# The first two modulation chunks as plain float32 products with the weights stationary

## The chip, the core and the metric

The kernel runs on one core of a Trainium2 chip. Its engines are TensorE (PE, matrix products, with PEld for its weight loads), VectorE (DVE), ScalarE (ACT), GpSimd (POOL) and SyncE (SP, which here issues transfers). The metric is the device time of one execution in microseconds (us).

## The reference, cut to what matters

One layer of a hybrid backbone: a modulation vector is computed from the conditioning vector, the latent tokens (512 x 1024) and the context tokens (256 x 1024) are normalized and modulated with it, and everything else (attention, a gating MLP, gates, a retrieval of experts) works on the result.

```python
sh1, sc1, g1, sh2, sc2, g2 = jnp.split(
    (jax.nn.silu(c) @ ada_w[layer] + ada_b[layer])[:, None, :], ADA_CHUNKS, axis=-1)
csh1, csc1, cg1, csh2, csc2, cg2 = jnp.split(
    jax.nn.silu(c_ctx) @ ada_w[layer] + ada_b[layer], ADA_CHUNKS, axis=-1)
w = w_in[layer]
h = modulate(rmsnorm(x, norm1_g[layer]), sh1, sc1)
hc = modulate(rmsnorm(ctx, norm1_g[layer]), csh1, csc1)
q, k, v, gu, gv, ga, gb = jnp.split(h @ w, IN_SPLITS, axis=-1)
```

The change concerns the first two of the six parts of the modulation, sh1 and sc1 (each 1024 wide), for two vectors at once: silu(c) and silu(c_ctx). It is a product of 2 x 1024 with 1024 x 2048.

## The kernel before

The kernel computes float32 products in three reduced ones: each operand is split into hi (rounded to the format fp32r, in which PE takes one pass) and lo (the rest), and the helper `mm3` (lines 86 to 88) adds hi\*hi, hi\*lo and lo\*hi in PSUM. `split` (lines 82 and 83) makes the two: ACT rounds, DVE subtracts.

The first stage goes by eight chunks c of 128 channels. `load_ada` fetches for each chunk two tiles `raw` of 512 KB (128 x 4 x 256: four blocks of 128 input channels, and in each the 128 columns of sh1 and the 128 of sc1 of this chunk); 8 such buffers exist. `ada_first(c)` makes the chunk's modulation: it splits both tiles, and PE multiplies them as the moving operand (256 columns) with `s4` as the stationary one, in which columns 0 and 1 hold hi of the two vectors, 2 and 3 their lo, and the other 124 zeros. The result is a row tile with 4 used partitions; ACT copies it to SBUF (line 170), and two products with `fold` (line 173) turn it into columns and add the lo part. DVE adds the bias into `mod1` (line 174) and makes the scale `a1` (line 176).

Before that stage, x is loaded, normalized (`norm`, lines 237 and 239) and transposed by PE (line 302); ACT and DVE copy the transposes into `xT` in turn (lines 304 and 306). `mod_x` then makes hh and hl, the hi and lo of the modulated chunk (lines 264 to 266). For each chunk PE makes 12 products of 512 columns (`o_gu`, weights `wh`, `wl`) and 12 of 256 columns (half of `o_gv`, weights `vh`, `vl`). `ada_first(c + 2)` is a generator whose steps stand between the products of chunk c. Behind the stage stand the transposes of the context (line 250), the other half of `o_gv`, and the projections of v, k and q. `gate` is a copy of the last modulation on POOL, behind which POOL issues the loads of the other four parts of the modulation (`araw`); DVE multiplies those by itself (lines 202 and 204).

The order on each engine is not that of the code: the framework places each instruction by a timeline of its own, and each engine then runs its list in that order. SP issues the loads in its list's order, and a load waits there for its buffer.

Of the kernel before, what the change touches and what calls it, by code (L numbers as in the profile page):

```python
# [9 lines left out]
F32 = mybir.dt.float32  # L10
F32R = mybir.dt.float32r
# [4 lines left out]
AF = mybir.ActivationFunctionType  # L16
OP = mybir.AluOpType
# [4 lines left out]
P = 128  # L22
# [3 lines left out]
NC8 = D // P  # L26
# [17 lines left out]
def f(ap):  # L44
    return ap.bitcast(F32)


def body(tc, A, out):
    nc = tc.nc
    pe, dve, act, pool, sp = nc.tensor, nc.vector, nc.scalar, nc.gpsimd, nc.sync  # L50
    es = ExitStack()

    def pool_(stack, name, side="left", bufs=1):
        return stack.enter_context(tc.tile_pool(name=name, bufs=bufs, side=side, reuse_waits="tile"))
# [6 lines left out]
    def ps(tag, shape=(P, 512)):  # L61

        t = psp.tile([P, 512], F32, name="ps" + tag, bufs=4 if tag == "m" else 2)
        n = int(np.prod(shape[1:]))
        v = t[:shape[0], :n]
        if len(shape) == 3:
            v = v.rearrange("p (a b) -> p a b", b=shape[2])
        return v

    ident = const.tile([P, P], F32, name="ident")  # L70
# [10 lines left out]
    def split(raw, hi, lo, sub=dve):  # L81
        act.activation(hi, raw, AF.Copy)  # L82
        return sub.tensor_tensor(lo, raw, f(hi), op=OP.subtract)  # L83
# [21 lines left out]
    def t2(dt=F32):  # L105
        return tmp.tile([P, 512], dt, name="t2", bufs=8)
# [26 lines left out]
    def load_rows(src, t):  # L133
        x = t4()
        sp.dma_start(x, src[t * P:(t + 1) * P, :])
        return x
# [3 lines left out]
    sc = const.tile([P, NC8, 2], F32, name="sc")  # L140
# [7 lines left out]
    mod1 = const.tile([P, 16, 2], F32, name="mod1")  # L148
    a1 = const.tile([P, NC8, 2], F32, name="a1")

    def load_ada(c, i):
        raw = aw.tile([P, 4, 256], F32, name="raw", bufs=8)
        sp.dma_start(raw, A["ada01"][c, i])
        return raw

    def ada_first(c):

        bank = ps("x")
        row = bank[:, :256]
        for i in range(2):  # L160
            raw = raws[c].pop(0) if c in raws else load_ada(c, i)
            hi = aw.tile([P, 4, 256], F32R, name="hi", bufs=2)
            lo = aw.tile([P, 4, 256], F32R, name="lo", bufs=2)
            split(raw, hi, lo)
            for k in range(4):
                for w in (hi, lo):
                    pe.matmul(row, s4[:, 4 * i + k, :], w[:, k, :], start=(i + k == 0 and w is hi), stop=(i * k == 3 and w is lo))
            yield
        rs = t2()
        act.activation(rs[:, :256], row, AF.Copy)  # L170
        cps = bank[:, 256:260].rearrange("p (n x) -> p n x", n=2)
        for n in range(2):
            pe.matmul(cps[:, n, :], rs[:, n * P:(n + 1) * P], fold, start=True, stop=True)
        dve.tensor_tensor(mod1.rearrange("p (n c) x -> p n c x", n=2)[:, :, c, :], cps,
                          abc[:, 0:2, c:c + 1].to_broadcast([P, 2, 2]), op=OP.add)
        dve.tensor_scalar(a1[:, c, :], mod1[:, 8 + c, :], 1.0, ng[:, 0, c:c + 1], op0=OP.add, op1=OP.mult)
        yield
# [102 lines left out]
    cl = cx.tile([P, NC8, CTX], F32R, name="cl")  # L280
    eaw = ExitStack()
    aw = pool_(eaw, "aw", "right")

    s4 = aw.tile([P, NC8, P], F32R, name="s4")
    dve.memset(f(s4), 0.0)
    act.activation(s4[:, :, 0:2], sc, AF.Copy)
    dve.tensor_tensor(s4[:, :, 2:4], sc, f(s4[:, :, 0:2]), op=OP.subtract)
    fold = aw.tile([P, 2], F32, name="fold")
    dve.tensor_tensor(fold, ident[:, 0:2], ident[:, 2:4], op=OP.add)
    xs = [load_rows(A["x"], t) for t in range(2)]  # L290
    raws = {0: [load_ada(0, i) for i in range(2)]}
    xs += [load_rows(A["x"], t) for t in range(2, NT)]
# [14 lines left out]
    for _ in ada_first(0):  # L307
        pass
# [20 lines left out]
    for _ in ada_first(1):  # L329
        pass  # L330
    mod_x(xT, *lat_h, (1,))
    for c in range(NC8):
        if c % 2 == 0:
            wh, wl = wload(A["w_in"][3, c // 2])
        if c % 4 == 0:
            vh, vl = half_weights(4, 0, c // 4)
        if c == 3:
            cxs = [load_rows(A["ctx"], t) for t in range(CTX // P)]
            for x in cxs:
                norm(x, x)  # L340
        parts = ada_first(c + 2) if c < 6 else iter(())
        for t in range(NT):
            next(parts, None)
            ts = slice(t * P, (t + 1) * P)
            mm3(o_gu[t], hh[:, c, ts], hl[:, c, ts], wh[:, c % 2], wl[:, c % 2], c == 0, c == 7)
            gv_products(o_gv, c, vh, vl, t)
        if c < 6:
            mod_x(xT, *lat_h, (c + 2,))
# [7 lines left out]
    def proj_T(src, g, ins, n=4, sub=None, tags="mmmm"):  # L356

        o = [[ps(t, (P, w)) for t in tags] for _, _, w in ins[:1]]
        for _, _, w in ins[1:]:
            o.append([x[:, i, :] for x in [ps("x", (P, 2, w)) for _ in range(2)] for i in range(2)])  # L360
        last = 2 * n - 1
        for c, wh, wl in weights(src, g, n, sub=sub):
            for i, (rh, rl, _) in enumerate(ins):
                for b in range(4):
                    bs = slice(b * P, (b + 1) * P)
                    if i == 0:
                        mm3(o[i][b], wh[:, bs], wl[:, bs], rh[:, c, :], rl[:, c, :], c == 0, c == last)
                    else:
                        mm3(o[i][b], wh[:, bs], wl[:, bs], rh[:, c, :], rl[:, c, :], c == 0 and b % 2 == 0, c == last and b % 2 == 1, True)
        return o  # L370

    def proj_N(src, g, ins):

        o = [ps("m" if i < 4 else "x") for i in range(len(ins))]
        for c, wh, wl in weights(src, g):
            for i, (lh, ll, t) in enumerate(ins):
                ts = slice(t * P, (t + 1) * P)
                mm3(o[i], lh[:, c, ts], ll[:, c, ts], wh, wl, c == 0, c == 7)
        return o
# [56 lines left out]
    o = proj_N(A["w_in"], 2, lat_N + [(ch, cl, 0), (ch, cl, 1)])  # L436
# [24 lines left out]
    for i in range(0, 8, 2):  # L461
        o = ps("xu"[i // 2 % 2], (P, 2, 256))
# [6 lines left out]
    o, = proj_T(A["w_in"], 0, lat_T, tags="mmuu")  # L469
    ql = [t4().bitcast(F32R).rearrange("p (b m r c) -> p b m r c", b=2, m=NT, r=8) for _ in range(2)]  # L470
    for b in range(4):
        for i in range(2):
            src = o[b][HALF[i]].rearrange("p (r m c) -> p m r c", r=8, m=NT)
            hi = q2[i][HALF[i], b]
# [131 lines left out]
    for n in range(2):  # L606
        o, = proj_T(A["w_in"], 7 + n, lat_T, tags=("mmmm", "uuxx")[n])
# [9 lines left out]
    for n in range(2):  # L617
        for nm, src in (("a", A["w_pa"]), ("b", A["w_pb"])):
            o, = proj_T(src, n, [(*y2[nm], S)], n=2, tags={"a": "mmmm", "b": "uuxx"}[nm])
# [40 lines left out]
    o = proj_N(A["w_out"], 0, [(m_h, m_l, t) for t in range(NT)])  # L660
# [6 lines left out]
    for p in range(2):  # L667
        o = [ps("m"), ps("m")]
# [12 lines left out]
    for p in range(2):  # L681
        if p == 0:
            o = [x[:, i] for x in [ps("x", (P, 2, 256)) for _ in range(2)] for i in range(2)]
        else:
            o = [ps("m", (P, 256)) for _ in range(4)]
# [65 lines left out]
    for g in range(4):  # L751
        if g > 0:
            o, = proj_T(A["wq"], g, [(h2h, h2l, S)], sub=pool)
# [6 lines left out]
        for t in range(NT):  # L760
            o = ps("x" if g < 3 else "m", (P, 4, P))
# [24 lines left out]
    rs = pool_(ro, "rs", "right", bufs=2)  # L786
# [129 lines left out]
    for t in range(DT):  # L916
# [4 lines left out]
        for g in range(P // TG):  # L921
            stg = rs.tile([P, P, TG], F32, name="stg")
            for u in range(TG // TB):
# [15 lines left out]
                for v in range(2):  # L939
                    o = ps("m", (P, 4, P))  # L940
# [232 lines left out]
```

## Time and profile before

| | before |
|---|---|
| median of 3 runs | 1718.19 us (1715.9 to 1718.95) |
| the profiled execution's own time | 1715.57 us |
| its span | 1713.8 us |
| busy, share of the span | PE 97%, PEld 86%, DVE 78%, ACT 41%, POOL 29% |
| mean granted clock of PE | 0.988 of 2.4 GHz |

The span goes from the first to the last instruction. PE's busy time counts the modelled ends of pipelined products, so neighbouring products overlap in it; what a product costs in a dense stretch is the distance to the start of the next one. In a row of the timeline, "x4" means that four instructions follow each other, and the brackets say how long the engine was idle before and what ended that.

### The profile page before, as it was taken

Reading aid. Unit: us, or ns where it says so; the run is one execution under the profiler, and the core shown is the slowest. Engines: PE = TensorE matmul, PEld = TensorE weight load, DVE = VectorE, ACT = ScalarE, POOL = GpSimd, SP = SyncE. Lnnn points to the kernel's source line nnn. Section 1 sums busy time; section 2 is a strip of 40 time slices with the busy share of each in tenths; the row PEclk is TensorE's granted clock in tenths of the full one; section 3 lists DMA queues with packets and bytes.
Section 4 is the critical chain, followed back from the end, with each engine's and each line's share of the span. In section 5 each row is a group of like instructions: output and inputs, shape, how many; then the busy total and the mean of one; then the engine's idle time right before and its main releaser. Section 6 shows DMA issues by size and latency. Waiting matters only on the chain.

```text
span 1713.8 us, 24752 instructions
## 1 busy us (share of the span) xinstructions
PE 1658.1 (97%) x9033; PEld 1466.4 (86%) x9033; DVE 1329.3 (78%) x2619; ACT 705.9 (41%) x1106; POOL 494.6 (29%) x362
## 2 busy tenths in 40 slices
PE   7999999999999999999599999999999999999997
PEld 6888777888888989999588888888999999999886
DVE  8687666456779999999378788788777777777885
ACT  6532555532532456565233333333333333333333
POOL 0011100000332530000244444455454454444321
PEclk9999999999999999999799999999999999999999
DMA  9377522233511435676989999999998998997892
GB/s 355 131 247 247 160 81 74 98 112 109 197 62 39 139 120 209 223 264 229 343 309 353 341 339 344 318 338 338 338 325 291 323 340 286 330 328 272 287 315 85
DMA packets 160818, 413.11 MB, mean 241 GB/s; under 512 B 13432, under 2 KB 71288, under 8 KB 157496
## 3 DMA queue, kind: packets, MB, share of 16 engines
q1 hardware_dynamic: 116112, 253.17, 42.7%
q0 software_dynamic: 42480, 154.43, 25.8%
q10 hardware_dynamic: 2104, 3.93, 0.7%
q8 instruction: 70, 1.15, 0.3%
q14 instruction: 52, 0.43, 0.1%
HBM read 375.70 MB, written 35.78 MB: 240 GB/s over the span
## 4 chain that ended last, share of the span: by engine, by line
PE 76%; DVE 13%; DMA 5%; issue 4%; ACT 1%; SPq 0%; POOL 0%; DVEq 0%; POOLq 0%; ACTq 0%
PE psu L86 10%; PE psu L88 10%; PE psu L87 10%; PE psm L86 10%; PE psm L88 10%; PE psm L87 9%; PE psx L88 4%; PE psx L87 4%; PE psx L86 4%; PE psm L943 2%; DMA araw<-in_ada 2%; DMA wgt<-gad 1%; DVE z L712 1%; DVE i L714 1%; DVE i L711 1%
## 5 line engine op out<-in xcount | busy, mean ns | idle before, releaser
L88 PE MATMUL psu<-h2h,ulo 128*128 128x384 f32 x992 | 338.2, 342 | 3.5 <-DVE ulo L83 3.4
L86 PE MATMUL psu<-h2h,uhi 128*128 128x384 f32 x992 | 338.4, 341 | 2.7 <-ACT gact L859 2.6
L87 PE MATMUL psu<-h2l,uhi 128*128 128x384 f32 x992 | 336.9, 340 | 0.0
L1009 POOL DMA_INDIRECT gx<-in_peer_u,ex x128 | 190.3, 1487 | 244.3 <-DVE gj L1019 232.4
L82 ACT ACTIVATE uhi<-uraw 128x1024 fp32r<-128x1024 f32 x126 | 133.6, 1061 | 285.1 <-PE psu L87 245.3
L1009 POOL DMA_INDIRECT gx<-in_peer_v,ex x128 | 185.4, 1448 | 189.0 <-DVE acc L1024 139.1
L87 PE MATMUL psm<-vlo,wgh 128*128 128x512 f32 x504 | 199.3, 396 | 0.1
L88 PE MATMUL psm<-vhi,wgl 128*128 128x512 f32 x504 | 197.6, 394 | 1.1 <-DVE wgl L1000 1.1
L86 PE MATMUL psm<-vhi,wgh 128*128 128x512 f32 x504 | 175.0, 393 | 19.4 <-ACT wgh L999 18.4
L86 PEld LDWEIGHTS psu<-h2h,uhi 128*128 128x128 f32 x992 | 186.9, 188 | 6.8 <-ACT gact L859 3.3
L88 PEld LDWEIGHTS psu<-h2h,ulo 128*128 128x128 f32 x992 | 186.8, 188 | 4.6 <-DVE ulo L83 3.8
L87 PEld LDWEIGHTS psu<-h2l,uhi 128*128 128x128 f32 x992 | 186.9, 188 | 3.9
L999 ACT ACTIVATE wgh<-wgt 128x384 fp32r<-128x384 f32 x126 | 65.5, 524 | 296.3 <-issue 164.3
L83 DVE TENSOR_TENSOR vlo<-vraw,vhi 128x1024 fp32r<-128x1024 f32 x126 | 154.7, 1228 | 24.9 <-ACT vhi L82 24.6
L1000 DVE TENSOR_TENSOR wgl<-wgt,wgh 128x384 fp32r<-128x384 f32 x126 | 70.2, 557 | 130.5 <-ACT wgh L999 130.4
L1024 DVE SCALAR_TENSOR_TENSOR acc<-gx,wg,acc 128x1024 f32<-128x1024 f32 x128 | 163.8, 1280 | 0.0
L82 ACT ACTIVATE vhi<-vraw 128x1024 fp32r<-128x1024 f32 x126 | 132.0, 1047 | 65.9 <-DMA vraw<-in_peer_v 36.2
L1019 DVE SCALAR_TENSOR_TENSOR gj<-gx,h2n 128x1024 bf16<-128x1024 f32 x128 | 156.0, 1218 | 0.1
L83 DVE TENSOR_TENSOR ulo<-uraw,uhi 128x1024 fp32r<-128x1024 f32 x112 | 136.8, 1221 | 15.6 <-ACT uhi L82 12.3
L86 PEld LDWEIGHTS psm<-vhi,wgh 128*128 128x128 f32 x504 | 95.5, 190 | 38.0 <-ACT wgh L999 19.1
L82 ACT ACTIVATE whi<-wraw 128x1024 fp32r<-128x1024 f32 x60 | 63.6, 1062 | 121.0 <-PE psx L87 44.3
L88 PEld LDWEIGHTS psm<-vhi,wgl 128*128 128x128 f32 x504 | 95.0, 189 | 21.3 <-DVE wgl L1000 1.4
(383 smaller groups left out, 3360.2 us busy)
## 6 DMA issues: line engine op xcount, KB each, us to landing
vraw<-in_peer_v SPq DMA_DIRECT2D x126, 512.0 KB, 6.8
uraw<-in_ut SPq DMA_DIRECT2D x124, 512.0 KB, 5.6
wd<-stg SPq DMA_DIRECT2D x24, 1024.0 KB
wr<-wd SPq DMA_DIRECT2D x45, 512.0 KB, 10.1
araw<-in_ada POOLq DMA_DIRECT2D x32, 512.0 KB, 4.9
wraw<-in_w_in SPq DMA_DIRECT2D x24, 512.0 KB, 4.5
raw<-in_ada SPq DMA_DIRECT2D x16, 512.0 KB, 10.2
wraw<-in_wq SPq DMA_DIRECT2D x16, 512.0 KB, 3.4
```

The costliest lines, as they stand in the source:

```text
L82: act.activation(hi, raw, AF.Copy)
L83: return sub.tensor_tensor(lo, raw, f(hi), op=OP.subtract)
L86: pe.matmul(o, lh, rh, start=first, stop=False, skip_group_check=shared)
L87: pe.matmul(o, lh, rl, start=False, stop=False, skip_group_check=shared)
L88: return pe.matmul(o, ll, rh, start=False, stop=last, skip_group_check=shared).ins
L711: dve.max_index(idx[:, 0:8], val[:, 0:8], src)
L943: pe.matmul(o[:, x, :], eb_[:, 2 * v + x // 2, :, x % 2], oa[n][:, 2 * v + x // 2, :, x % 2], start=(n == 0), stop=(n == 1))
L999: act.activation(wh, w, AF.Copy)
L1000: last = dve.tensor_tensor(wl, w, f(wh), op=OP.subtract)
L1009: pool.indirect_dma_start(out=t, out_offset=None, in_=src, in_offset=bass.IndirectOffsetOnAxis(ap=ex[:, k:k + 1], axis=0))
L1019: dve.scalar_tensor_tensor(junk, u, 1.0, h2n, op0=OP.mult, op1=OP.mult, accum_out=actg[:, i:i + 1])
L1024: dve.scalar_tensor_tensor(acc, v, wg[:, i:i + 1], acc, op0=OP.mult, op1=OP.add)
```

## The change

`ada_first` no longer splits the raw tiles. The raw float32 weights become the stationary operand, 128 x 128 at a time, and the two vectors `sc` (128 x 2 for each block) the moving one, as plain float32 products: 16 for each chunk, 8 for the half of sh1 and 8 for that of sc1. The result has the form of columns already, so the row's copy and the fold go, and with them `s4` and `fold`. The first tile is held until the second is there.

```diff
     def ada_first(c):
 
-        bank = ps("x")
-        row = bank[:, :256]
+        o = ps("x", (P, 2, 2))
         for i in range(2):
             raw = raws[c].pop(0) if c in raws else load_ada(c, i)
-            hi = aw.tile([P, 4, 256], F32R, name="hi", bufs=2)
-            lo = aw.tile([P, 4, 256], F32R, name="lo", bufs=2)
-            split(raw, hi, lo)
-            for k in range(4):
-                for w in (hi, lo):
-                    pe.matmul(row, s4[:, 4 * i + k, :], w[:, k, :], start=(i + k == 0 and w is hi), stop=(i * k == 3 and w is lo))
-            yield
-        rs = t2()
-        act.activation(rs[:, :256], row, AF.Copy)
-        cps = bank[:, 256:260].rearrange("p (n x) -> p n x", n=2)
+            if i == 0:
+                held_ = raw
+                yield
         for n in range(2):
-            pe.matmul(cps[:, n, :], rs[:, n * P:(n + 1) * P], fold, start=True, stop=True)
-        dve.tensor_tensor(mod1.rearrange("p (n c) x -> p n c x", n=2)[:, :, c, :], cps,
+            for i, raw_ in enumerate((held_, raw)):
+                for k in range(4):
+                    pe.matmul(o[:, n, :], raw_[:, k, n * P:(n + 1) * P], sc[:, 4 * i + k, :], start=(i + k == 0), stop=(i * k == 3))
+            if n == 0:
+                yield
+        dve.tensor_tensor(mod1.rearrange("p (n c) x -> p n c x", n=2)[:, :, c, :], o,
                           abc[:, 0:2, c:c + 1].to_broadcast([P, 2, 2]), op=OP.add)
...
-    s4 = aw.tile([P, NC8, P], F32R, name="s4")
-    dve.memset(f(s4), 0.0)
-    act.activation(s4[:, :, 0:2], sc, AF.Copy)
-    dve.tensor_tensor(s4[:, :, 2:4], sc, f(s4[:, :, 0:2]), op=OP.subtract)
-    fold = aw.tile([P, 2], F32, name="fold")
-    dve.tensor_tensor(fold, ident[:, 0:2], ident[:, 2:4], op=OP.add)
```

The framework's order changes with it on PE, DVE, ACT and SP in the first stage; behind it each engine's list is the same but for a few moves. Line numbers of the new kernel are smaller by 4 to 11.

First place: PE from the first instruction to the products of x's transposes. t_121, t_123, t_129 and t_131 are the four normalized tiles of x. Before:

```order
L302 MATMUL psm<-ident,t_121 128x128 x4
L167 MATMUL psx<-hi,s_115 128x256
L302 MATMUL psm<-ident,t_123 128x128 x4
L167 MATMUL psx<-lo,s_115 128x256
L167 MATMUL psx<-hi,s_115 128x256
```

And with the change, where the tiles of x are called t_115, t_117, t_123 and t_125:

```order
L167 MATMUL psx<-sc,raw 128x2 x4
L291 MATMUL psm<-ident,t_115 128x128 x4
L167 MATMUL psx<-sc,raw 128x2 x7
L291 MATMUL psm<-ident,t_117 128x128 x4
L167 MATMUL psx<-sc,raw 128x2 x9
L291 MATMUL psm<-ident,t_123 128x128 x4
L291 MATMUL psm<-ident,t_125 128x128 x4
L167 MATMUL psx<-sc,raw 128x2 x10
```

The products of the modulation now stand ahead of the transposes; the 10 in the last row are chunk 1's, of which two more stand behind the other 16 transposes.

Second place: DVE from the last normalization to the first residual of hh. Before (line 83 is a split's residual, 306 a copy of transposes, 265 and 266 make hl of chunk 0):

```order
L83 TENSOR_TENSOR lo<-raw,hi 128x1024
L239 TENSOR_SCALAR t_131<-t_131,rstd_159 128x1024
L83 TENSOR_TENSOR wlo<-wraw,whi 128x1024
L306 COPY xT<-psm 128x512 x2
L83 TENSOR_TENSOR wlo<-wraw,whi 128x1024
L265 TENSOR_SCALAR t_252<-xT,a_96,mod_95 128x512
L306 COPY xT<-psm 128x512
L83 TENSOR_TENSOR lo<-raw,hi 128x1024
L306 COPY xT<-psm 128x512
L266 TENSOR_TENSOR hl<-t_252,hh 128x512
```

And with the change (the copy is line 295, hl 261 and 262, the bias 170, the scale 172):

```order
L235 TENSOR_SCALAR t_125<-t_125,rstd_153 128x1024
L170 TENSOR_TENSOR mod_95<-psx,abc 128x2x2
L172 TENSOR_SCALAR a_96<-mod_95,ng 128x2
L83 TENSOR_TENSOR wlo<-wraw,whi 128x1024
L295 COPY xT<-psm 128x512
L83 TENSOR_TENSOR wlo<-wraw,whi 128x1024
L295 COPY xT<-psm 128x512
L261 TENSOR_SCALAR t_234<-xT,a_96,mod_95 128x512
L262 TENSOR_TENSOR hl<-t_234,hh 128x512
```

The residuals of the raw tiles are gone; the two residuals of the w_in weights stay, and a copy of xT stands behind each of them.

Third place: PE among the products of chunk 2, with the change:

```order
L167 MATMUL psx<-sc,raw 128x2 x8
L86 MATMUL psm<-whi,hh 128x512
L87 MATMUL psm<-wlo,hh 128x512
L88 MATMUL psm<-whi,hl 128x512
L86 MATMUL psu<-whi,hh 128x256
L87 MATMUL psu<-wlo,hh 128x256
L88 MATMUL psu<-whi,hl 128x256
L167 MATMUL psx<-sc,raw 128x2 x8
L86 MATMUL psm<-whi,hh 128x512
```

A chunk's 16 plain products stand in two bursts of 8 with the six w_in products of one token tile between them; before, 16 products of 256 columns and a fold stood there.

## Rows read from the trace of the kernel before

**Rows 1.** Page, part 4: the chain that ended last, shares of the span.

```profile
PE 76%; DVE 13%; DMA 5%; issue 4%; ACT 1%; SPq 0%; POOL 0%; DVEq 0%; POOLq 0%; ACTq 0%
```

**Rows 2.** Groups by line and form, 0 to 80 us (busy us, mean ns).

```profile
L173 PE MATMUL psx<-fold,t 128*128 128x2 f32 x32 | 4.1, 234 | 0.5 <-ACT t L170 0.5
...
L83 DVE TENSOR_TENSOR lo<-raw,hi 128x1024 fp32r<-128x1024 f32 x16 | 19.4, 1222 | 1.5 <-DMA raw<-in_ada 0.9 <-ACT hi L82 0.5
...
L306 DVE COPY xT<-psm 128x512 f32<-128x512 f32 x4 | 2.7, 689 | 0.0
```

**Rows 3.** Timeline of PE, a stretch without waits: start us, us, engine, line, operation.

```profile
34.07 0.28 PE L167 MATMUL psx<-hi,s 128*128 128x256 f32 x1
...
35.70 0.40 PE L86 MATMUL psm<-whi,hh 128*128 128x512 f32 x1
...
36.17 0.28 PE L86 MATMUL psu<-whi,hh 128*128 128x256 f32 x1
36.29 0.28 PE L87 MATMUL psu<-wlo,hh 128*128 128x256 f32 x1
```

**Rows 4.** Timeline of ACT, then PE: the start of the w_in products.

```profile
16.93 1.06 ACT L82 ACTIVATE whi<-wraw 128x1024 fp32r<-128x1024 f32 x1 [0.45 <-DMA wraw<-in_w_in]
...
19.21 1.97 PE L302 MATMUL psm<-ident,t 128*128 128x128 f32 x16 [0.47 <-ACT xT L304]
...
21.36 0.39 PE L86 MATMUL psu<-whi,hh 128*128 128x256 f32 x1
```

**Rows 5.** Timeline of DVE, then PE: waits, and the stage's end.

```profile
28.66 0.70 DVE L266 TENSOR_TENSOR hl<-t,hh 128x512 fp32r<-128x512 f32 x1
...
51.74 0.49 PE L87 MATMUL psu<-wlo,hh 128*128 128x256 f32 x2
53.10 0.50 PE L88 MATMUL psm<-whi,hl 128*128 128x512 f32 x1 [0.87 <-DVE hl L266]
...
57.88 0.51 PE L86 MATMUL psm<-whi,hh 128*128 128x512 f32 x1 [0.37 <-ACT hh L264]
...
73.00 0.60 PE L250 MATMUL psx<-ident,t 128*128 128x128 f32 x4
```

**Rows 6.** Timeline of PE, products with one and two columns.

```profile
21.93 0.51 PE L173 MATMUL psx<-fold,t 128*128 128x2 f32 x4
22.30 0.47 PE L86 MATMUL psm<-whi,hh 128*128 128x512 f32 x1
22.61 0.39 PE L87 MATMUL psm<-wlo,hh 128*128 128x512 f32 x1
...
106.64 0.95 PE L220 MATMUL psu<-ones,t 128*128 128x1 f32 x8
107.44 0.49 PE L87 MATMUL psm<-wlo,hh 128*128 128x512 f32 x1
107.77 0.40 PE L88 MATMUL psm<-whi,hl 128*128 128x512 f32 x1
```

**Rows 7.** Page, part 6 (KB, us to landing), then timeline of DVE.

```profile
raw<-in_ada SPq DMA_DIRECT2D x16, 512.0 KB, 10.2
...
66.57 0.16 DVE L174 TENSOR_TENSOR mod<-psx,abc 128x4 f32<-128x4 f32 x1 [0.94 <-PE psx L173]
```

**Rows 8.** Timeline of DVE, then PE, 148 to 175 us.

```profile
153.02 1.37 DVE L450 SCALAR_TENSOR_TENSOR k<-psm,k 64x512 fp32r<-64x512 f32 x2 [2.92 <-ACT k L449]
...
170.97 1.54 DVE L204 SCALAR_TENSOR_TENSOR t<-araw,sc,t 128x512 f32<-128x512 f32 x2 [1.78 <-DMA araw<-in_ada]
...
174.25 0.94 PE L466 MATMUL psx<-t,t 128*128 128x128 f32 x6 [2.61 <-DVE gu L467]
```

**Rows 9.** Windows: stretch, length, busy us of each engine, PEclk, DMA share, GB/s.

```profile
176.00:178.00 2.00, 2.00 (x7) 1.52 (x6) 0.00 (x0) 0.56 (x1) 0.00 (x0) 0.50 0.18 72
```

**Rows 10.** Timeline of PE, its first products.

```profile
11.00 0.42 PE L167 MATMUL psx<-lo,s 128*128 128x256 f32 x1
11.21 0.41 PE L167 MATMUL psx<-hi,s 128*128 128x256 f32 x1
```

## The prediction

> **What bounds the kernel now.** I read the chain of waits first [rows 1]: 76% of the span ends in work of TensorE (PE), so a microsecond added to or taken from PE's line of work counts until something shows that it doesn't. The change touches the first 85 us only, so I read the groups of the first 80 us next, then PE's timeline there. In the groups [rows 2] the reader should see that one chunk's modulation costs DVE two residuals of 1.222 us (16 in all, 19.4 us), and PE 16 products of 256 columns (hi and lo) and one fold. The groups' means are no prices for PE, since its instructions overlap; its price is the distance between starts. Two products of 512 columns start 0.47 apart, so 0.235 each; 14 products of the rows 34.07 to 35.70 take 1.63, so 0.1165 each; a 256-column product of the branch weights costs 0.12, taken as 0.1175 [rows 3].
>
> Is PE the bound of the stretch that the change rewrites? From the first product with w_in (21.36) [rows 4] to the four transposes behind chunk 7 (73.00) [rows 5] is 51.64 us. In it lie 96 products of 512 columns (22.6), 96 of 256 (11.3), 95 hi and lo products (11.1), 7 folds (3.1, priced below) and 6 transposes at 0.11 (0.65): 48.7. So PE waited 2.9 us in all; the two largest waits are about 1.0 before 53.10, for hl of chunk 4 behind DVE's queue, and 0.6 before 57.88, for hh [rows 5]. DVE and ACT are late now and then, but PE is 94% of this stretch.
>
> **The change part by part.** *The split, row and fold go.* DVE loses 16 residuals and the clearing of s, ACT 16 roundings and 8 copies of the row. From 21.36 on that work lies beside PE's and is worth only PE's waits, 2.9 us. In the new order DVE reaches every hl before PE does: hl of chunk 1, behind the third weight residual in both orders, began at 28.66 with seven residuals of the modulation ahead of it [rows 5] and now comes sooner, while PE is through with chunk 0 at about 29.2 (21.4, 4.2 of w_in products, 16 plain products at 3.6); I take the full 2.9 (lower end 2.0, if the wait for the second gate-weight tile, whose buffer is freed only by chunk 3, stays in part).
>
> *PE's products.* For the six chunks after the first two, 95 hi and lo products (11.1) and 7 folds (3.1) become 96 plain products. The trace shows such a product: the fold has 16 instructions and 32 records, so two passes each, with a weight load per pass [rows 2]. A fold's four passes start at 21.93, the next product at 22.30, and the one after that 0.31 later, not 0.235: 0.445 in all, 0.111 a pass. Eight passes with one column, 106.64 to 107.77 less a 512-column product's 0.235, are 0.895, 0.112 a pass [rows 6]. The difference of the two, 0.45 for four more passes, is 0.1125, and I take that: a pass costs as much as a whole 256-column product, because a new set of weights goes in for each. The new stationary tile is 128 x 128, as there. 96 x 2 x 0.1125 = 21.6 us. Bounds: 0.0925, if the delay behind a burst (0.08) is paid once and not per pass (17.8 us); 0.1165, the hi and lo spacing (22.4 us); a load that overlapped nothing would cost more, but in no row of the bursts does it.
>
> *The start.* The order of DVE shows what decides: before PE's first w_in product come both weight residuals and two copies of xT. The second weight tile lands at 16.93, and ACT's rounding takes 1.06 [rows 4]. DVE has then done the first residual and the copy of chunk 0 (0.69 [rows 2]) by about 18.2; the second residual ends at 19.35, the copy of chunk 2 at 20.0. Only then are PE's banks free for the transposes of chunks 6 and 7 (8 x 0.109, from the 16 of the row at 19.21: 1.97 less the last one's tail [rows 4]), to 20.9, and behind them stand two products of chunk 1 (0.45): 21.35. It was 21.36. So the faster norm of the last x tile, now without residuals ahead of it, is lost behind the weights' landing; its worth is taken as 0 (between +0.5 and -1.0). The products of chunks 0 and 1 themselves cost nothing here, since they run while PE waits for x and the weights.
>
> *The raw tiles* are held until PE has used both halves. The ninth load waits for chunk 0's products (about 14), the eleventh for chunk 1's (21.4). A tile takes 10.2 us from issue to landing [rows 7], and the two are needed inside chunks 2 and 3, at about 38 and 46: hidden, with 14 us to spare. gate, which starts the other modulation's loads, hangs on chunk 7's modulation, at 66.57 so far [rows 7]; the last burst now ends inside chunk 5, at about 65. Nothing follows from that, as long as those loads don't set the end (a rival).
>
> *Sum.* 22.6 + 11.3 + 21.6 = 55.5 after, against 51.64 - 0.65 = 51.0 before (the 6 transposes move behind in the new order, at equal cost): PE leaves this stage 4.5 us later. By the bounds 0.7 to 5.3, and 6.2 with 0.9 of waits left.
>
> *Behind it.* PE is dense from 73 to 171. DVE idles 2.92 us before 153.02 until PE's key projection lets ACT go on, and from there the line runs over DVE's key copies and the next loads of the modulation to DVE at 170.97 and PE's wait of 2.61 before 174.25 [rows 8]. All of that starts from PE, so it moves with PE. Every engine's order behind the first stage is the same but for a few moves, and I found nothing tied to the clock on the wall. So +4.5 reaches the end: 1715.57 + 4.5 = 1720.1 against the profiled execution. That one was 0.15% under the median of the runs, 1718.19; on the median's scale the forecast is 1722.7 us. The three runs differ by 3 us, so about 0.2% (3.4 us) is what a measurement of this kernel can tell from no change.
>
> **The rivals.** *The shift is swallowed at 174.25 (0.19).* The chain of waits runs between 96 and 172 over the modulation's loads, not over PE. If these loads set the moment 174.25, PE's 4.5 first fills its wait of 2.61, and then the slow stretch behind it (granted clock 0.50 at 176 to 178 [rows 9]), worth some 1.7, falls away too: +0.2, so 1718.4. Against it speaks DVE's wait for PE at 153.02; for it, that the last wait of DVE (1.78 before 170.97) is for a load.
>
> *The clock (0.12).* PE's first products start 0.215 apart [rows 10], twice the later distance: PE begins at 1.2 GHz and rises at about 11.6, after 3 us of transposes and 256-column products. After the idle 2.61 us it fell again [rows 8, 9]. The new start has two-column passes and few transposes, and each chunk has two bursts of 16 such passes with 1 us of wide products between them; no row shows a burst above 8. If they don't keep the clock up, 32 products and 32 transposes of the start cost 0.215 a pass, 13.8 + 6.9 = 20.7 us from about 7.6, so chunk 0 begins 6.9 late; and two or three falls later at some 1.7 each add 4: 4.5 + 6.9 + 4 = +15, 1733. A single fall in the stage gives 1724.5. For the bursts the rows speak against it: the clock stayed up over the fold and the 8 passes.
> The Trainium skill, "TensorE: Matmul & The Clock Gate", section on HAM oscillation, tells the clock as following how busy the array has been and names idle gaps as what drops it; the rows at 174 agree, and no run here shows whether narrow passes count as busy.
>
> *Faster (0.07).* A pass is cheaper in long bursts, because its load is drawn ahead of the pass before. The point that decides is where the new passes cost what goes: 11.1 + 3.1 + 2.9 = 17.1 us over 192 passes, 0.089. At 0.06 the sum is -5.6: 1712.6. For it: a two-column pass moves next to nothing. Against it: 4 and 8 passes cost 0.111 and 0.112, with no fall.
> The skill's same page, section "Back-to-back issue gap", gives some 60 cycles for up to 64 columns, which as an estimate would be 192 x 0.025 = 4.8 us and a gain of 12; its section on LDWEIGHTS gives 128 / 1.2 = 107 ns for a load, with which the trace's 0.112 agrees.
>
> **How the numbers follow.** The forecast has 0.62. Between its bounds and with the runs' spread about a quarter of it lies under 0.2%. Slower: 0.62 x 0.77 + 0.12 = 0.60; same: 0.19 + 0.14 = 0.33; faster 0.07. The range leaves out the faster case and the clock's full price (0.19 together): from 1717.5, the swallowed shift less 1, to 1728, the upper bound of the sum (6.2) with one or two falls of the clock. The forecast's own range is 1719 to 1725.
>
> **What would show it.** Right: 256 records of two columns, spaced about 0.1125 in their bursts, 1.8 us a burst; the first w_in product at 21 to 22; no PE wait above 0.3 from there to chunk 7; chunk 7's last product about 4.5 later; PE's wait near 174 shifted to about 179 with its length unchanged. Wrong: spacing under 0.09 (faster); a wait near 174 that shrinks (swallowed); 0.215 between passes or 0.425 between 512-column products behind the first 12 us (the clock); a first w_in product well before 20, which would mean that DVE's residuals, not the weights' landing, held the start.

## The result and the profile after

The changed kernel takes 1745.21 us (median of 4 runs, 1739.47 to 1746.06), the kernel before 1718.57 beside it: ratio 1.0144, 95% interval 1.0128 to 1.0159, so 26.6 us slower. The profiled execution took 1746.06 us, 30.5 more than that of before (1715.57). The forecast was 1722.7 us: it named the direction, and lay 22.5 us too low.

The new kernel's chain that ended last, shares of the span, answers to [rows 1]: PE's share rose by two hundredths.

```profile
PE 78%; DVE 10%; DMA 5%; issue 5%; ACT 1%; POOL 0%; SPq 0%; POOLq 0%; DVEq 0%; ACTq 0%
```

The new kernel's plain products among the groups by line and form, 0 to 80 us; they stand for the three groups of [rows 2]. 256 records are 128 products of two passes.

```profile
L167 PE MATMUL psx<-sc,raw 128*128 128x2 f32 x256 | 36.4, 271 | 7.9 <-DMA raw<-in_ada 7.9
```

The new kernel's timeline of PE, answering to [rows 3 to 6], [rows 8] and [rows 10] (start, length, operation, and in brackets the idle time before):

```profile
7.90 1.84 PE L167 MATMUL psx<-sc,raw 128*128 128x2 f32 x8 [7.90 <-DMA raw<-in_ada]
9.60 1.09 PE L291 MATMUL psm<-ident,t 128*128 128x128 f32 x4
...
19.66 4.27 PE L167 MATMUL psx<-sc,raw 128*128 128x2 f32 x20
23.79 3.65 PE L291 MATMUL psm<-ident,t 128*128 128x128 f32 x16
...
27.95 0.56 PE L86 MATMUL psu<-whi,hh 128*128 128x256 f32 x1
...
37.20 1.84 PE L167 MATMUL psx<-sc,raw 128*128 128x2 f32 x16
38.91 0.48 PE L86 MATMUL psm<-whi,hh 128*128 128x512 f32 x1
...
49.73 0.77 PE L86 MATMUL psm<-whi,hh 128*128 128x512 f32 x1
50.30 0.63 PE L87 MATMUL psm<-wlo,hh 128*128 128x512 f32 x1
50.73 0.63 PE L88 MATMUL psm<-whi,hl 128*128 128x512 f32 x1
...
86.50 0.60 PE L246 MATMUL psx<-ident,t 128*128 128x128 f32 x4
...
138.50 1.84 PE L216 MATMUL psu<-ones,t 128*128 128x1 f32 x8 [3.71 <-DVE t L200]
...
196.11 2.08 PE L455 MATMUL psx<-t,t 128*128 128x128 f32 x8 [3.58 <-DVE gu L456]
```

Four places are to be read here.

**The start.** From 7.90 PE works without a pause, but the 8 passes to 9.60 start 0.21 apart, as do the 20 from 19.66 and the 16 transposes from 23.79: 1.2 GHz for 20 us. Chunk 0's first w_in product starts at 27.95 (21.36 [rows 4]): 6.6 late.

**The stage.** In the burst at 37.20, 16 passes take 1.71, so 0.107 each. At 49.73 the 512-column products, wide ones, start 0.57 and 0.43 apart (0.235 in [rows 3]): the clock is down again, with no idle time before it. The four transposes behind chunk 7 stand at 86.50 (73.00 [rows 5]): 13.5 late, so the stage itself gave 6.9.

**The sums of the other modulation.** Before 138.50 PE waits 3.71 for DVE. In the kernel before it did not wait there.

**The end.** At 196.11 PE is 21.9 later than at 174.25 [rows 8]. By the span's end it is 30.5.

Three windows of the new kernel show the granted clock (the sixth value from the left behind the five engines, PEclk; as in [rows 9]):

```profile
48.00:58.00 10.00, 10.00 (x64) 9.21 (x63) 5.35 (x12) 1.41 (x3) 0.00 (x0) 0.83 0.14 46
...
66.00:70.00 4.00, 4.00 (x17) 3.48 (x17) 1.63 (x4) 0.82 (x1) 0.00 (x0) 0.57 0.52 192
...
136.00:146.00 10.00, 7.50 (x24) 6.35 (x25) 6.71 (x11) 2.11 (x4) 1.98 (x4) 0.66 0.93 323
```

Lost are 0.17 x 10 = 1.7, 0.43 x 4 = 1.7 and 0.34 x 10 = 3.4 us. Of the last, some 0.3 lie in the idle time before 138.50: from there to 146.00 the column reads 0.58, so 0.42 x 7.5 = 3.1 of PE's work. The column reads 1.00 over the whole start, though: ahead of the clock's first rise only the distances tell.

Where the first 21.9 us come from: 6.6 at the start; 3.4 by two stretches of low clock in the stage; 3.5, the rest of the stage's 6.9, put down to the products; 3.7 by the wait for the sums; 3.1 by the low clock behind it; 1.0 by the longer wait before 196.11. That is 21.3.

Why the sums come late stands on DVE and POOL. The new kernel's timeline of DVE; `t<-araw,sc` (line 198, before 202) is the other modulation's first step:

```profile
104.89 0.55 DVE L252 TENSOR_SCALAR t<-psx,a,mod 128x256 f32<-128x256 f32 x1 [0.38 <-ACT ch L247]
105.35 0.48 DVE L198 TENSOR_SCALAR t<-araw,sc 128x512 f32<-128x512 f32 x1
```

In the kernel before, the same step on DVE:

```profile
83.70 0.48 DVE L202 TENSOR_SCALAR t<-araw,sc 128x512 f32<-128x512 f32 x1
```

The fourth of that modulation's loads waits for a buffer that the first two steps free. POOL's issue of it, in the new kernel:

```profile
107.46 0.53 POOL L183 DMA_DIRECT2D araw<-in_ada  x1 [14.73 <-DVE t L200]
```

and in the kernel before:

```profile
87.64 0.53 POOL L187 DMA_DIRECT2D araw<-in_ada  x1 [17.15 <-DVE mv L423]
```

PE is 13.5 us late at the end of the stage, this load 19.8. The step stands behind the context's chunk 6 on DVE (104.89), whose transposes the new order puts further back on PE.

The last 8.6 us arise in the late stages, where PE waits 8.9 us in place of 1.9. The new kernel's waits of PE from 900 us on (us in total, times, longest):

```profile
PE psm L86 <- ACT vhi L82: 5.1, 1, 5.1
PE psm L86 <- ACT wgh L988: 3.0, 1, 3.0
PE psm L88 <- DVE wgl L989: 0.8, 1, 0.8
```

and of the kernel before, from 880 us on:

```profile
PE psm L88 <- DVE wgl L1000: 1.1, 1, 1.1
PE psm L86 <- ACT vhi L82: 0.8, 1, 0.8
```

### The profile page after: what moved, and what is told of

The parts are those of the page before. It is cut to its first block, busy times and chain, and to the rows that moved or that the text cites. A ratio compares the mean times of both kernels' runs of the same rounds, so it can differ in the third digit from the quotient of the medians.

```text
span 1744.3 us, 24881 instructions
## 1 busy us (share of the span) xinstructions
PE 1681.9 (96%) x9129; PEld 1490.2 (85%) x9129; DVE 1310.4 (75%) x2600; ACT 689.3 (40%) x1081; POOL 494.6 (28%) x362
## 4 chain that ended last, share of the span: by engine, by line
PE 78%; DVE 10%; DMA 5%; issue 5%; ACT 1%; POOL 0%; SPq 0%; POOLq 0%; DVEq 0%; ACTq 0%
PE psm L86 10%; PE psm L87 10%; PE psm L88 10%; PE psu L86 10%; PE psu L88 10%; PE psu L87 9%; PE psx L86 4%; PE psx L87 4%; PE psx L88 4%; DMA araw<-in_ada 2%; PE psm L932 2%; PE psx L167 2%; DVE z L701 1%; DVE i L703 1%; DVE i L700 1%
## 5 line engine op out<-in xcount | busy, mean ns | idle before, releaser
L86 PEld LDWEIGHTS psm<-vhi,wgh 128*128 128x128 f32 x504 | 96.0, 191 | 44.6 <-ACT wgh L988 21.3
```

Source lines behind the costliest of these rows:

```text
L86: pe.matmul(o, lh, rh, start=first, stop=False, skip_group_check=shared)
```

## The experiments

My theories were three: (A) two-column passes neither raise PE's clock nor always hold it, which gives the late start and the two falls; (B) the plain products cost some 3.5 us of their own; (C) the moved step of the other modulation makes PE wait at 138.50. The rivals: the start is late by the order on PE; the sums are late because everything is; the late waits are the change's.

| run | median us | kernel before beside it | ratio, 95% interval |
|---|---|---|---|
| cols64 | 1727.89 (5 runs) | 1719.16 | 1.0039 to 1.0080 |
| araw_early | 1730.52 (4) | 1719.16 | 1.0053 to 1.0098 |
| cols64_araw_early | 1723.07 (9) | 1719.16 | 1.0011 to 1.0036 |
| before_late | 1718.99 (10) | 1719.16 | 0.9986 to 1.0010 |
| warm | 1734.35 (4) | 1719.67 | 1.0062 to 1.0108 |
| warm_cols64_araw | 1719.28 (12) | 1719.67 | 0.9988 to 1.0016 |
| start_only | 1721.76 (10) | 1719.67 | 0.9997 to 1.0034 |
| stage_only | 1731.40 (4) | 1719.67 | 1.0057 to 1.0109 |
| warm26 | 1735.21 (4) | 1716.29 | 1.0093 to 1.0157 |
| warm26_cols64_araw | 1719.22 (12) | 1716.29 | 0.9994 to 1.0029 |
| warm26_cols128_araw | 1718.56 (12) | 1716.29 | 0.9997 to 1.0031 |
| after_again | 1742.12 (4) | 1716.29 | 1.0093 to 1.0163 |
| before_again | 1718.46 (8) | 1718.28 | 0.9990 to 1.0018 |
| before_delay | 1733.06 (4) | 1718.28 | 1.0056 to 1.0096 |

Single runs of the kernel before went from 1711.3 to 1723.0 us, so a few us between medians of few runs say little.

### Wider passes

```diff
+SW = 64
...
-        o = ps("x", (P, 2, 2))
+        o = ps("x", (P, 2, SW))
...
-                    pe.matmul(o[:, n, :], raw_[:, k, n * P:(n + 1) * P], sc[:, 4 * i + k, :], ...
+                    pe.matmul(o[:, n, :], raw_[:, k, n * P:(n + 1) * P], scw[:, 4 * i + k, :], ...
```

`scw` holds `sc` in its first two columns and zeros in the others; the lines that make it are left out here.

> The new kernel with 64 moving columns in place of two in the 128 plain products (columns 3 to 64 are zeros and their results are not used); passes, weight loads and the order on every engine up to the retrieval stage stay. Theory: two columns leave TensorE at its lower clock at the start (passes 0.215 apart up to 28.8 us) and let it fall twice in the stage. Then wide passes raise the clock as the old products did, at 11 to 14 us: chunk 0's first w_in product comes back from 27.95 to 21 to 23, no granted clock under 1 from there to chunk 7, and the time falls by 6 + 2 x 1.3 = 8 to 9, to about 1736 to 1737 (1733 to 1739). Rival: the start is late because 32 products stand ahead of the transposes in TensorE's order, whatever the clock: the first w_in product stays at 27 to 28 and the time at 1744 to 1747. Second rival: a pass with 64 columns costs more than one with two: bursts of 16 passes above 1.9 us (1.72 so far).

With 64 columns, PE's timeline:

```profile
22.01 1.92 PE L295 MATMUL psm<-ident,t 128*128 128x128 f32 x16
...
24.13 0.36 PE L87 MATMUL psu<-whi,hh 128*128 128x256 f32 x1
...
79.22 0.60 PE L247 MATMUL psx<-ident,t 128*128 128x128 f32 x4
```

The 16 transposes now take 1.9 and not 3.65: the clock rose inside the 20 passes ahead of them, and the first w_in product comes 3.8 earlier, not 5 to 7. From 24 to 85 us the granted clock is 1.00 throughout. From the first w_in product to the four transposes it is 79.22 - 24.13 = 55.09 us, where the kernel before has 51.64: 3.45 for the products. Theory A holds for the stage and in part for the start. The order on PE is the same in this stage, so the rival falls. The time fell by more than expected, in part because the wait for the sums shrank too (to 1.6, with no low clock behind it); the late wait for wgh (3.0 above) isn't in this trace either.

### The moved step

```diff
-                part = t2()
+                part = t2() if j else tmp.tile([P, 512], F32, name="t2f", bufs=1)
...
+                with tc.issue_after(cts[(2, 2, 4)[min(len(steps), 2)]].ins):
```

`cts` are the context's temporaries on DVE. Two more edges put the context's chunk 4 behind the second step and the batch-norm statistics behind the third and fourth.

> The new kernel with the first two steps of the other modulation on VectorE put ahead of the context's chunk 4, and the next ones between the batch-norm statistics; the first partial sum gets a buffer of its own, so that it need not wait for the context's temporaries. Theory: in the new kernel this step came 21.7 us later than before (83.70, then 105.35) while TensorE was only some 13 to 15 us late, which held back the chain of loads and made TensorE wait 3.7 us at 134.4 and then run at half its clock for 6.8 us. Then the step runs near 95 to 97, the fourth load is issued near 98 and not at 107.5, the wait near 134 and the low clock behind it go, and the time falls by 3.7 + 3.4 = 7, to about 1738 (1736 to 1740). Rival: those loads are late because they start later as a whole (76.33 in place of 66.80) and the step's place decides nothing: the wait stays above 3 us, the time at 1744 to 1747.

The fourth load is issued at 97.80 in place of 107.46, and of PE's waits between 80 and 190 us one is left, the one before the gelu's transposes:

```profile
PE psx L459 <- DVE gu L460: 2.6, 1, 2.6
```

The transposes that stood at 196.11 come at 188.30, 7.8 earlier: 7 expected. The median fell by more, 14.7, with a wide spread (1723 to 1736); the trace is that of the fastest execution, and its late waits are short (0.8 for vhi, none for wgh). In the kernel before, the opposite edit:

```diff
+    tc.add_manual_dep(steps[0].ins, aggr.ins.name, ...)
```

> The kernel before with one edit: the first step of the other modulation stands behind the last batch-norm aggregate on VectorE, as in the new kernel, and not ahead of the first statistics. No product is changed. Theory: it runs at about 91 in place of 83.70, the fourth load of that modulation is issued about 5 us later (87.64 so far), TensorE gets a wait of 1 to 4 us before the sums of that modulation at 120 to 130, and if that wait drops the clock, some 3 us more: +2 to +7, 1721 to 1726. Rival: the loads have slack and nothing waits: 1718 to 1719.

Its fourth load is issued at 91.79, 4.2 late, and PE doesn't wait for the sums: the rival was right. What counts is the load's distance from PE's own place. From the four transposes behind chunk 7 to the fourth load it is 14.6 us in the kernel before and in the three runs below that keep its order there (`start_only`, `before_again`, `before_delay`), 18.1 in `before_late`, and 21.0 in all six traces with the step where the new order has it (two of the new kernel, `cols64`, `stage_only`, `warm`, `warm26`). PE waits for the sums in these six and in none of the other five. So 3.5 us more cost nothing and 6.3 more bring a wait; putting the step back removes it. Theory C needs this threshold, and the place alone doesn't set the wait's length, which is 1.3 to 4.3 in the six.

Both edits of the new kernel together, with no new one:

> Both edits together. If the two causes are separate, the gains add: 8.5 + 7 = 15 to 16 off 1745, to 1729 to 1731, of which 4.5 to 6 above the kernel before are the products' own price and the rest lies in the later stages. If the loads of the other modulation only wait because the whole first stage is late, the sum is no more than that of the wider columns alone, about 1736.

1723.07 is better than the 1729 to 1731 expected, but the two measured gains don't add: 17.3 and 14.7 off 1745.2 would be 1713. In its trace, that of the slowest of the nine executions, the start was as late as ever (first w_in product 28.15). The clock's rise in the start is thus not the same in each execution, even with 64 columns: the start's products and their order are those of `cols64`.

### PE kept busy ahead of the start

```diff
+    wz = aw.tile([P, 512], F32R, name="wz")
+    dve.memset(f(wz), 0.0)
+    wo = ps("u")
+    for _ in range(12):
+        pe.matmul(wo, wz[:, 0:P], wz, start=True, stop=True)
```

> The new kernel with 12 products of 512 columns (zeros, results not used) on TensorE ahead of its first product, from about 2 to 8 us, while it waits for x and the first raw tile. Theory: the start is late only because two-column passes leave TensorE at its lower clock. Then passes start 0.107 apart from the first one on, chunk 0's first w_in product comes at 21 to 22.5 (27.95 in the new kernel) and the time falls by about 6, from 1745 to 1738 to 1740. If a clock that is up falls again over the narrow passes of the start, 0.215 returns between passes before 20 us and the product comes at 24 to 27. Rival: the place of the 32 products in the order makes the start late: 27 to 28 with passes 0.107 apart and TensorE waiting. The two falls in the stage stay in all cases.

This missed, and tells much. The timeline of PE:

```profile
1.64 4.65 PE L283 MATMUL psu<-wz 128*128 128x512 f32 x12 [1.64 <-DVE wz L280]
8.71 1.84 PE L167 MATMUL psx<-sc,raw 128*128 128x2 f32 x8 [2.43 <-DMA raw<-in_ada]
...
30.35 0.56 PE L86 MATMUL psu<-whi,hh 128*128 128x256 f32 x1
```

The products raised the clock, PE then idled 2.43 for the raw tile, and the clock fell. Over the narrow passes and transposes that follow, without a pause, it stayed at 0.50 from 10 to 30 us, and it came back at 36, among chunk 0's wide products. (The median still fell; in this kernel's trace the late waits for vhi and wgh were 0.9 and 0.7, more on which below.) With `range(26)` there is no idle time:

> The new kernel with 26 wide products of zeros ahead in place of 12, so that TensorE has work until the first raw tile lands at about 8.7 and no idle time lies between (with 12, it idled 2.4 us, the clock fell at 9, and passes stayed 0.215 apart to 30 us). Theory: narrow passes don't raise a clock that is down, and the start costs what it does because it is down. If they keep one that is up, passes stand 0.107 apart up to the first w_in product, which comes at 21.3 to 22.5 and not at 28 to 30, and the time is 12 x 0.5 = 6 to 8 us under that with 12 products (1734.4) : 1726 to 1729. If they let it fall again (as in two bursts of the stage), 0.215 returns between 10 and 20 us, the first w_in product comes at 24 to 28: 1730 to 1735.

```profile
1.64 8.30 PE L283 MATMUL psu<-wz 128*128 128x512 f32 x26 [1.64 <-DVE wz L280]
...
11.27 5.26 PE L167 MATMUL psx<-sc,raw 128*128 128x2 f32 x32
...
18.45 4.69 PE L167 MATMUL psx<-sc,raw 128*128 128x2 f32 x22
...
26.45 0.38 PE L167 MATMUL psx<-sc,raw 128*128 128x2 f32 x2
26.69 0.36 PE L86 MATMUL psu<-whi,hh 128*128 128x256 f32 x1
```

Windows of the same kernel:

```profile
8.00:13.00 5.00, 5.00 (x40) 4.69 (x38) 3.91 (x9) 0.59 (x2) 0.00 (x0) 1.00 1.02 401
13.00:20.00 7.00, 7.00 (x36) 7.00 (x36) 4.87 (x9) 3.84 (x5) 0.00 (x0) 0.50 1.05 399
```

PE is busy all the time and the clock falls from 2.4 to 1.2 GHz at 13 us, inside a row of 32 two-column passes. That is the second branch of what was expected, and the second half of theory A by itself: no wait takes part. The first half needs a limit: the clock was up again at 26.6, ahead of the first w_in product, after 13.6 us of nothing but such passes and transposes. So they can end a low stretch, only late. With 64 columns behind the 26 products, and the step early:

> All three remedies with 26 products ahead. With 12 the start was still as late (first passes 0.215 apart, first w_in product 31.9 in its order) and the time 1719.3, as the kernel before. If the 64-column passes keep the clock up from the start, the first w_in product comes at 21.3 to 22.5, 6 us or more of start come back, and the time is 1712 to 1714, 0.3% under the kernel before; the plain products' price (3 to 3.5 in the stage) remains. If the start is hidden by something behind it, 1718 to 1720.

```profile
9.72 0.78 PE L168 MATMUL psx<-scw,raw 128*128 128x64 f32 x6
...
11.21 3.68 PE L168 MATMUL psx<-scw,raw 128*128 128x64 f32 x32
...
20.98 0.49 PE L87 MATMUL psu<-whi,hh 128*128 128x256 f32 x2
...
75.16 0.60 PE L249 MATMUL psx<-ident,t 128*128 128x128 f32 x4
```

The same 32 passes take 3.5 and not 5.1, the first w_in product stands at 20.98, and the granted clock is 1.00 from 8 to 85 us. The transposes behind chunk 7 come at 75.16, 2.2 later than before. With the 26 products ahead in both kernels, the clock stayed up with the wider passes and fell with the narrow ones; the early step acts only behind the stage. The time, 1719.22 against 1716.29, can't be told from the kernel before; 1712 to 1714 was a miss: nothing beyond the losses came back.

And with 128 columns:

> As warm26_cols64_araw, with 128 moving columns in place of 64. If a pass's price is that of its weight load, bursts of 16 passes take 1.72 as with two columns and the time equals that with 64 (within 2 us). If the moving columns set it at this width, bursts take over 1.8 us and 12 bursts cost 1 us or more.

```profile
24.91 1.95 PE L168 MATMUL psx<-scw,raw 128*128 128x128 f32 x16
26.62 0.48 PE L87 MATMUL psm<-whi,hh 128*128 128x512 f32 x1
```

A burst of 16 passes takes 1.71 (24.91 to 26.62), the time is 1718.56: the price of a pass is the same with 2, 64 and 128 columns.

The same with 12 products:

> The new kernel with all three remedies: the 12 wide products ahead, 64 moving columns, the first steps of the other modulation early. The two remedies together without the products ahead took 1723.1 with a start that was still 6.9 us late in the profiled execution. If the start comes back, 1723 - 6 = 1717 (1715 to 1719), so that the plain products' own price (10.3 - 6.9 = 3.4 us between the first w_in product and the stage's end) is all that stands against the old way. If the start was the only cause left above the kernel before, 1719; if the start's 6.9 was partly swallowed later, 1720 to 1723.

1719.28, equal to the kernel before. Its trace shows the idle time and the fall of `warm` (clock 0.51 from 8 to 30 us), but that execution had a mean granted clock of 0.981 and took 1725.18; the other eleven had 0.984 to 0.990. Mostly, then, the clock probably did not stay down so long. In this trace 64 columns did not raise it before 32 us.

### The two parts apart

```diff
-    for _ in ada_first(0):
+    for _ in (ada_new if 0 in NEWC else ada_first)(0):
```

> The kernel before with chunks 0 and 1 alone in the new way; chunks 2 to 7 keep split, hi and lo products and fold. Theory: the late start alone is worth what the first w_in product is late, 6 to 7 us, less up to 1.5 where TensorE's waits inside the stage (2.9 us in all) shrink because VectorE is ahead: 1718.6 + 5 to 7 = 1723.5 to 1725.5; no fall of the clock in the stage. Rival, the reading of the prediction (products of the first two chunks cost nothing): first w_in product at 21 to 22, 1718 to 1720.

> The kernel before with chunks 2 to 7 in the new way and chunks 0 and 1 in the old one. The first w_in product stays at 21 to 22. Theory: the plain products cost 3 to 4.5 us between there and the stage's end, falls of the clock there 1.6 each (none to two), and the other modulation's first step, which again stands behind the batch-norm aggregates in this order, 1 to 7 us behind 130: 1718.6 + 3 to 4.5 + 0 to 3 + 1 to 7 = 1723 to 1731. Rival: without the late start nothing is lost behind the stage, 1721 to 1723.

With chunks 0 and 1 alone in the new way (`NEWC = range(2)`), the transposes behind chunk 7 stand at 78.11, 5.1 late, as theory A has it; but the median is only 2.1 above the kernel before, over 1714.7 to 1729.8 us, inconclusive. The profiled execution took 1727.81, the second longest of the ten, so its trace is not the usual one. With chunks 2 to 7 alone, 1731.40: the clock was at 0.66 in four stretches of 5 us (26 to 31, 37 to 42, 54 to 59 and 71 to 76), 1.7 us lost in each, and PE waited 1.3 for the sums. Less these four falls, the stage takes 84.03 - 23.12 - 6.8 = 54.1, 2.5 more than before. Falls in the stage thus need no late start. (The start of this kernel is the old one; 23.12 and not 21.36, since the clock was down there from 17 to 20 us.)

### The late waits

> The new kernel itself, for a second trace. In its first one 6.9 us of the 30.5 came only behind 1637 us of the kernel before (a wait of 5.5 for vraw, then 6.8 us at half the clock) and 3.0 at 903, where the variants with the same first 100 us had less. If these belong to the change (through the time at which the last stages' loads run), they stand again in this trace, within 1 us, and the median is 1744 to 1746. If they are chance of one execution, this trace has them at another place or not at all, at 1736 to 1740, while the first 200 us (first w_in product near 28, stage's end +13, wait for the sums near 134 of 3 to 4) repeat.

In the second trace of the new kernel the first w_in product and the transposes behind chunk 7 stand at

```profile
27.60 0.56 PE L86 MATMUL psu<-whi,hh 128*128 128x256 f32 x1
...
94.23 0.60 PE L246 MATMUL psx<-ident,t 128*128 128x128 f32 x4
```

so the stage took 66.6 us, 8 more than in the first trace: 512-column products still start 0.43 apart at 30 us, and the clock falls again at 56 and 80. The wait for the sums was 4.3, for vhi 3.7, for wgh 2.3. The runs spread from 1731.8 to 1750.3. The size of the clock's part differs between executions; in both traces it lies in the start and in the stage.

> The kernel before itself, for a second trace. In its first one TensorE waited 0.8 us for vhi and 1.1 for wgl behind 880 us; with the change 5.1 and 3.7 in two traces for vhi, 3.0 and 2.3 for wgh, and a low clock behind them. If these waits come with some executions of any kernel, this trace of the kernel before has a wait of 2 to 5 us at one of the two places, at 1718 to 1722 in all. If the change causes them, it has none above 1.2, at 1714 to 1719.

A second trace of the kernel before, PE's waits from 880 us on:

```profile
PE psm L86 <- ACT wgh L999: 2.3, 1, 2.3
PE psm L88 <- DVE wgl L1000: 0.8, 1, 0.8
PE psm L86 <- ACT vhi L82: 0.7, 1, 0.7
```

So the wait for wgh comes without the change too. Vhi stays at 0.7. The same trace has the first w_in product here:

```profile
22.93 0.39 PE L86 MATMUL psu<-whi,hh 128*128 128x256 f32 x1
```

The clock was down from 17 to 20 us in it, and from 16 to 19 in `before_late`, where the product stands at 22.44. The first trace of the kernel before (21.36) had a favourable start, and against these two the new kernel's 27.95 is 5.0 and 5.5 late.

Last, a shift without the change: the diff of `warm` on the kernel before, with 115 products.

> The kernel before with 115 wide products of zeros ahead, so that TensorE's first transposes come at about 30.5 us and not at 8.5; no other product is changed. From there 32 transposes and chunk 0's 16 products at the full clock (3.5 and 3.7, the latter in part behind) put the first w_in product at 35 to 38, 14 to 17 late. If a shift of the first stage reaches the end one to one, the time is 1717 + 14 to 17 = 1731 to 1734, and the waits behind 880 stay as in the kernel before (under 1.2 each). If a shift by itself brings the later waits (loads of the last stages that run at other moments against TensorE), vhi and wgh show 2 to 5 us and the time is 3 to 8 more: 1735 to 1742. If the shift is swallowed, 1717 to 1725.

The four transposes come at 88.64, 15.6 late, and the median is 14.8 above the kernel before: a shift of the first stage reaches the end nearly one to one. (The framework's order of the start moved with it, and the first w_in product stands at 40.21, where 35 to 38 was expected.) Vhi shows 2.3. Over all traces, the wait for vhi is at most 1.1 in the kernel before (twice), before_late, araw_early and the five changed kernels with wide products ahead, and 2.3 to 5.1 in the other seven, the new kernel's two among them. What sets it is open.

## Why the prediction was wrong

**"I take the full 2.9" of PE's waits in the stage: right.** PE has no wait between 28 and 90 us in the new kernel; the 2.9 us of waits are gone, as forecast.

**"A pass costs as much as a whole 256-column product", at 0.1125: right.** Measured are 0.107 from pass to pass and 0.08 once behind a burst (38.91 to 39.22 is 0.31 and not 0.235, as behind a fold): 192 x 0.107 + 12 x 0.08 = 21.5, forecast 21.6. Less its falls, the stage took 53.5 to 55.5 us in the runs, forecast 55.5; the low values are those of orders that put up to 16 of the 192 passes ahead of the first w_in product. This was the forecast's whole sum, and for the stage it stands. In the time it can't be seen: with the other losses undone, the ratio to the kernel before is 1.0011 (0.9994 to 1.0029), which holds the forecast's +4.5 (1.0026) and no change alike.

**"The start ... its worth is taken as 0": wrong, 6.6 us.** The step that failed is "The products of chunks 0 and 1 themselves cost nothing here, since they run while PE waits": that holds at 2.4 GHz only (first w_in product at 20.98 in `warm26_cols64_araw`). At 1.2 GHz, PE is the bound of the start: it worked without a pause from 7.90 on, and chunk 0 came 6.6 late, 5.0 to 5.5 against the other two traces of the old start. The rival "the clock" had worked out exactly this: 6.9 late (measured 6.6), two or three falls at 1.7 each (two), +15 in all, of which 13.5 showed behind chunk 7; its 1733 still lay 12 us too low, by the sums and the late waits. It got a chance of 0.12 because "for the bursts the rows speak against it". But [rows 6] show 4 and 8 passes between wide products, and the new bursts have 16, the start up to 20. The Trainium skill, "TensorE: Matmul & The Clock Gate", section "What's actually happening", counts the clock's warm-up as a time and not as a number of products. Here that time was not the same for all products: 3 us of transposes and 256-column products in the kernel before (8.5 to 11.6), 20 us of two-column passes and transposes in the new one, without a pause in either. The Trainium skill's section on HAM oscillation, on the same page, names idle gaps as what drops the clock; in `warm` it fell in one of 2.43 us, and in `warm26` without any.

**"Every engine's order behind the first stage is the same but for a few moves": wrong in what it concluded, 7 to 8 us.** One of the moves was the first step of the other modulation, behind which four waits follow: DVE's step, POOL's fourth load, the sums, PE at 138.50. The prediction followed the modulation's loads only as a rival that would swallow time. `araw_early` takes the wait and the low clock behind it away; `before_late` shows that the place matters only beyond a slack.

**"So +4.5 reaches the end": the mechanism is right** (`before_delay`: 15.6 gives 14.8). "PE's wait near 174 ... with its length unchanged" was not quite so: it grew from 2.61 to 3.58.

**The other rivals.** *Swallowed at 174.25*: no, the stage's shift passed that place in full. *Faster*, under 0.089 a pass: no, 0.107.

**The late waits** (8.6 us of the 30.5 in the first trace) were not foreseen. Wgh comes in the kernel before as well; vhi is not settled. The first profiled execution of the kernel before was a favourable one for them, as for the start.

## What to carry to other kernels

A plain product that brings new weights costs 0.107 us a pass here, whether it moves 2 or 128 columns. Padding it with zero columns cost PE nothing, and over the padded passes a clock that was up stayed up; one that was down they did not always raise sooner (`cols64` did, `cols64_araw_early` and `warm_cols64_araw` did not). A clock that is low at the start makes work count that seemed to lie in idle time: work out a start at both levels and believe the rows only for bursts as long as the new ones. And of an order that is "the same but for a few moves", follow each move to the queue that waits for it.

## What was unexpected in the hardware

TensorE's clock went from 2.4 to 1.2 GHz in the middle of uninterrupted work, when that work was two-column passes (`warm26`, at 13 us), and over the same passes with 64 columns it stayed up. Once down, it stayed down over 20 us of such passes and fp32 transposes in `warm` (0.50 from 10 to 30 us), and rose after 13.6 us of them in `warm26`.
The page's clock column reads 1.00 ahead of the first rise, when the distances (0.21 a pass, 0.43 for 512 columns) show 1.2 GHz.
